# Decoder trunk: keys first where attention begins, DVE and ACT in a written order there, and one weight scaling tied behind the last branch readings

## The chip, the core and the metric

The kernel runs on one core of a Trainium2 chip. The metric is device time of one execution in microseconds (us). Five engines run their own instruction streams and wait for each other by semaphores: PE (TensorE, matmuls), DVE (VectorE), ACT (ScalarE), POOL (GpSimd) and SP (SyncE, which issues most of the DMAs).

## The reference, cut to what matters

One layer on x of 512 x 1024, in float32:

```python
h = _rmsnorm(x, norm1_g[l]) * (1.0 + scale1) + shift1
proj = h @ w_in[l]
qa, ka, va, qd, kd, vd, ga, gd = jnp.split(proj, points, axis=-1)
out_a = _sliding_window_attention(qa, ka, va, sinks, slopes_swa)      # 8 heads, 2 key heads, window 128
out_b = _diff_attention(qd, kd, vd, lam, lam_init, subln_g, slopes_diff)
merged = sigmoid(ga) * (out_a @ w_branch_swa) + sigmoid(gd) * (out_b @ w_branch_diff)
x = x + gate1 * (merged @ w_out)
x = x + gate2 * _conv_ffn(rmsnorm2(x), ...)                           # gated MLP, causal convolution
out = _rmsnorm(x, final_g)
```

(The call of attention and the lines from `merged` on are shortened here.)

## The kernel before

Every float32 operand of a projection is split in two parts that PE multiplies fast: a high part, which ACT makes as a cast, and a low part, which DVE makes as a subtraction of the high part from the original (`split`, L104; `evac`, L399). A product then takes three matmuls (high by high, high by low, low by high). For weights, `split_pair` (L97) takes a raw tile of 128 x 1024 and gives `_h` and `_l` out of small rings of buffers; a new raw load waits until an earlier raw tile has been split.

**The first projection** (`mm_k`, L344, `product`, L333) runs over eight blocks k of the model dimension. PE keeps eight sums of 128 x 512 in its eight PSUM banks all the while: the keys `aka` (0), two of the four query sums `aqa0` (1) and `aqa1` (2), the differential values `av0` (3), `av1` (4), `av2` (6) and `av3` (7), and the sliding-window values `ava` (5). In the last k the three matmuls of each sum stand together, so that the sums are complete one after the other, in the order of the tuple in `mm_k`.

**Reading the sums out.** `keep_v(i)` splits one value sum into `vvh` (ACT) and `vvl` (DVE). Keys and queries are 64 wide, and two heads lie in one sum, in its lower and upper 64 partitions. They are stored so that scores are two matmuls over 128 partitions: `stack` (L410) puts a query's high part into its own half of `qa` (ACT, L415) and the low part into the other half (DVE, L418); for `ka`, each half holds high parts twice (L443, four ACT casts) and a low part twice (L445, two DVE subtractions, then L448, two ACT copies). `vaT` (L449) is a plain copy. A stretch between `man.enter_context(tc.manual_schedule(...))` and `man.close()` keeps the written order on DVE and ACT; elsewhere a scheduler sets it from its estimate and from priorities, and `tc.issue_after(x)` keeps what is written inside it behind x.

**What PE does there.** PE's order is written out: `fill(n)` (L483) runs n steps of a queue of projections, three matmuls each, and between them stand scores (`swa_scores`, L524, named `sw`), transposes and value products. The first two projections in the queue are the other two query sums (`add_q`, L599; matmuls L108 to L110, sums `pqa2` and `pqa3`, weights `wqa2` and `wqa3`), then heads of the differential attention (`pq0` with `w2_0`). `SWA_FILL` (L36) says how many steps stand in each gap. A score's maximum is taken by DVE (L545, `mx`), the softmax is ACT's (L557 to L560), its divisor DVE's, `pva` (L459) transposes `vaT` in a bank that a value sum held. `nm` (L556) is the maximum, scaled, that the exponentials need.

**The output projection.** Each branch is multiplied by its weights in `add_merge` (L893); the sum of the differential branch is `pB0` to `pB7`, and DVE reads it in L913 (`tdall`), adds the other branch (L914) and splits the result into `mg..h` and `mg..l`. The output projection's eight sums `oc` (L1186 to L1190) take over banks, one of them that of `pB7`. Its weights `wo0` to `wo7` come through `load_rows` (L958): a load, a scaling by the gate on DVE (L961) and a split.

Of the kernel before, what the change touches and what calls it, by code (L numbers as in the profile page):

```python
# [8 lines left out]
F32 = mybir.dt.float32  # L9
F32R = mybir.dt.float32r  # L10
AF = mybir.ActivationFunctionType
# [3 lines left out]
P = 128  # L15
# [17 lines left out]
STAT_LAG = 10  # L33
NORM_LAG = 16
VA_AT = 5
SWA_FILL = (1, 2, 6, 2, 2, 2, 2, 3)  # L36
DIFF_FILL = (3, 2, 4, 2)
NCOL = 161

# [4 lines left out]
def kernel(  # L44
# [47 lines left out]
    def raw_tile(shape, name):  # L92
        return wp.tile(shape, F32, tag="raw", bufs=4, name=name)
# [250 lines left out]
    def mm_k(k, part):  # L344
        if k < KT - 1:
            for i in (3, 4, 6, 0, 1, 2, 5, 7) if k < 2 else range(8):
                product(k, i, part)
        elif part == 0:
            for i in (3, 0, 1, 5, 2, 4, 6, 7):
                for p in range(3):  # L350
                    product(k, i, p)

# [54 lines left out]

    halves = ((lower, upper), (upper, lower))

    def stack(dst, src, scale, js=(0, 1), soon=True):  # L410
        with tc.high_priority(offset=HP) if soon else ExitStack():
            sc = [scale if isinstance(scale, float) else scale[own] for own, _ in halves]
            for j in js:
                own = halves[j][0]
                nc.scalar.activation(dst[own, j], src[own], AF.Copy, scale=sc[j])  # L415
            for j in js:
                own, other = halves[j]
                nc.vector.scalar_tensor_tensor(  # L418
                    dst[other, j], src[own], sc[j], dst[own, j].bitcast(F32), ALU.mult, ALU.subtract
                )  # L420
# [10 lines left out]
    vv = [big.tile([P, DIFF_HEADS, S], F32R, tag=f"vv{g}", name=f"vv{g}") for g in "hl"]  # L431
    vaT = big.tile([P, S], F32, tag="sq2", name="vaT")

    def keep_v(i):
        t = TOKENS[i] * P
        evac(*(v[:, :, t : t + P] for v in vv), acc[i].rearrange("p (h d) -> p h d", d=P))

    man = ExitStack()
    man.enter_context(tc.manual_schedule(engines={nc.vector.engine, nc.scalar.engine}))
    keep_v(3)  # L440
    for j, (own, other) in enumerate(halves):
        for to in (own, other):
            nc.scalar.copy(ka[to, j, 0], acc[0][own])  # L443
    for j, (own, _) in enumerate(halves):
        nc.vector.tensor_sub(ka[own, j, 1], acc[0][own], ka[own, j, 0].bitcast(F32))  # L445
    stack(qa[:, 0], acc[1], qsc[:, 0:1])
    for j, (own, other) in enumerate(halves):
        nc.scalar.copy(ka[other, j, 1], ka[own, j, 1])  # L448
    nc.scalar.copy(vaT, acc[5])  # L449
    man.close()  # L450
    stack(qa[:, 1], acc[2], qsc[:, 1:2], soon=False)
    keep_v(4)
    keep_v(6)
    keep_v(7)

    def turn_va():
        pv = tbank("pva")
# [6 lines left out]
        nsink = cpool.tile([P, 8], F32, name="nsink")  # L464
        nc.vector.tensor_scalar_mul(nsink, sink, -1.0)


    def load_tile(n, name):
        r = raw_tile([P, KT, P], name)
        nc.sync.dma_start(r, w_tiles[n])  # L470
        return split_pair(r, [P, KT, P], name)

    man = ExitStack()
    man.enter_context(tc.manual_schedule(engines={nc.tensor.engine}))
# [124 lines left out]
    def add_q(i):  # L599
        def q(wts):  # L600
            o = fbank(f"pqa{i}")
            yield from steps(o, wts, hT, KT)
            stack(qa[:, i], o, qsc[:, i : i + 1])

        units.append((lambda: load_tile(TILE_QA + i, f"wqa{i}"), q))

    def add_head(h):
        def q(wts):
# [155 lines left out]

    pairs, firsts, scored, probs, aTs = {}, {}, {}, {}, {}
    ada = ada_rows()
    add_q(2)
    add_q(3)
    add_head(0)
    add_head(1)  # L770
    with tc.issue_after(tiles[KT - 1].ins):
        prefetch(1)
        fill(SWA_FILL[0])
    swa_scores(0, 0)
    with tc.issue_after(pairs[0].last.ins):
# [89 lines left out]
    tds = {}  # L865

    g1b = gpart(4, [P, D], "g1b")
    g1c, s2c, a2c, g2c = (late_mod[:, 8 * i : 8 * i + 8] for i in range(4))
# [24 lines left out]
    def add_merge(j):  # L893
# [14 lines left out]
        def branch(wts):  # L908
            o = sbank(f"pB{j}")
            rhs = [[vv[b][:, k] for k in range(4)] for b in range(2)]  # L910
            yield from steps(o, wts, rhs, 4, cl=slice(j % 2 * P, j % 2 * P + P))
            td = tds[j]
            nc.vector.scalar_tensor_tensor(td, td, 1.0, o, ALU.add, ALU.mult)  # L913
            nc.vector.tensor_add(td, td, ta[:, j])  # L914
            split(mgh[j], mgl[j], td)

# [887 lines left out]
```

## Time and profile before

| | us |
|---|---|
| median of 3 runs (lowest, highest) | 684.09 (683.17, 686.54) |
| the profiled execution | 684.12 |
| its span | 682.3 |
| PE busy | 670.2 |
| DVE busy | 567.7 |
| ACT busy | 403.7 |

The profile is one execution on the chip. The span runs from the first to the last recorded instruction. A timeline row reads: start in us, duration in us, engine, line of the kernel, operation, output<-input, and, in brackets, how long the engine stood idle before it and whose work ended that. A row with x4 stands for four instructions of one kind in a row. Names are cut of their numbers in the trace (`wqa` is `wqa2` or `wqa3`). Matmuls are pipelined, so that one starts before the last has ended: what a matmul costs is read from the distance between starts.

### The profile page before, as it was taken

The page shows a single profiled execution, that of the slowest core. Times are in us where ns is not written, and L with a number is a line of the kernel's source. Part 1 is how long each engine was busy: PE and PEld are TensorE (multiplying, and loading weights), DVE is VectorE, ACT ScalarE, POOL GpSimd, SP SyncE. Part 2 cuts the span into 40 slices and gives each one's busy share as a digit, 9 for nine tenths or more (in the row PEclk, how much of TensorE's full clock was granted, in tenths as well). Part 3 has the DMA queues.
Part 4 walks back from the last instruction along what each step waited for, and adds up shares of the span by engine and source line. Part 5 has one row for each costly group of instructions (what it writes and reads, how often), then busy time and mean ns, then how long its engine had stood idle before and what let it go on. Part 6 is the DMA issues. An engine that isn't in the chain of part 4 may idle for free.

```text
span 682.3 us, 10835 instructions
## 1 busy us (share of the span) xinstructions
PE 670.2 (98%) x4053; PEld 594.3 (87%) x4053; DVE 567.7 (83%) x1049; ACT 403.7 (59%) x703; POOL 66.1 (10%) x74
## 2 busy tenths in 40 slices
PE   8999999999999999999999999999999999999995
PEld 7887787888888888878899999999999998888884
DVE  5986887789887388973689998888888999979997
ACT  6678878565654233332498565565556666656665
POOL 2000000001000000000020120111110003440300
PEclk9999999999999999999999999999999999999998
DMA  9961322354254289757473998787867658996903
GB/s 359 418 218 35 124 62 94 123 155 130 93 180 155 80 291 304 263 128 270 144 125 97 215 218 213 185 194 178 215 159 189 149 185 189 195 204 188 166 1 124
DMA packets 71077, 119.68 MB, mean 175 GB/s; under 512 B 3952, under 2 KB 47728, under 8 KB 71024
## 3 DMA queue, kind: packets, MB, share of 16 engines
q1 hardware_dynamic: 52960, 95.04, 41.7%
q0 software_dynamic: 17776, 23.60, 21.4%
q8 instruction: 32, 0.52, 0.3%
q10 hardware_dynamic: 288, 0.34, 0.2%
q14 instruction: 21, 0.17, 0.1%
HBM read 116.87 MB, written 2.10 MB: 174 GB/s over the span
## 4 chain that ended last, share of the span: by engine, by line
PE 79%; DVE 8%; DMA 6%; issue 3%; ACT 3%; ACTq 0%; DVEq 0%
PE up L1130 33%; PE dc L1733 11%; DMA wgd<-in_w_tiles_dram 3%; PE av L342 3%; DMA wo<-in_w_out_dram 2%; PE oc L1186 2%; PE oc L1187 2%; PE oc L1190 2%; PE pga L108 2%; PE pga L110 2%; PE pga L109 2%; PE sd L637 2%; PE aqa L339 1%; PE pq L108 1%; PE pk L108 1%
## 5 line engine op out<-in xcount | busy, mean ns | idle before, releaser
L1130 PE MATMUL up<-t,m_whi 128*128 128x256 f32 x512 | 93.1, 283 | 0.0
L1130 PEld LDWEIGHTS up<-t,m_whi 128*128 128x128 f32 x512 | 79.9, 192 | 0.0
L1130 PE MATMUL up<-t,m_wlo 128*128 128x256 f32 x256 | 72.4, 283 | 0.0
L1130 PE MATMUL up<-bh,p_whi 128*128 128x256 f32 x232 | 65.7, 283 | 0.0
L1130 PE MATMUL up<-bl,p_whi 128*128 128x256 f32 x232 | 65.7, 283 | 0.0
L1130 PE MATMUL up<-bh,p_wlo 128*128 128x256 f32 x232 | 65.7, 283 | 0.0
L1130 PEld LDWEIGHTS up<-t,m_wlo 128*128 128x128 f32 x256 | 49.2, 192 | 0.0
L1130 PEld LDWEIGHTS up<-bh,p_whi 128*128 128x128 f32 x232 | 44.5, 192 | 0.0
L1130 PEld LDWEIGHTS up<-bl,p_whi 128*128 128x128 f32 x232 | 44.5, 192 | 0.0
L1130 PEld LDWEIGHTS up<-bh,p_wlo 128*128 128x128 f32 x232 | 44.5, 192 | 0.0
L1033 POOL DMA_DIRECT2D s<-in_w_up_dram x21 | 27.0, 1365 | 158.2 <-DMA s<-in_w_up_dram 110.3
L1061 ACT CAST m_whi<-s 128x1024 fp32r<-128x1024 f32 x31 | 32.4, 1046 | 15.7 <-DVE s L1055 9.1
L732 DVE CUSTOM_DVE_ANT_0 ra<-ra,csb 128x1024 f32<-128x1024 f32 x32 | 38.6, 1221 | 1.6 <-DMA ra<-in_w_ada_t_dram 1.5
L1065 DVE TENSOR_TENSOR m_wlo<-s,m_whi 128x1024 fp32r<-128x1024 f32 x31 | 37.8, 1219 | 1.3 <-ACT m_whi L1061 1.3
L1130 PE MATMUL up<-t,p_whi 128*128 128x256 f32 x176 | 32.2, 283 | 0.0
L662 ACT ACTIVATE sd<-sd,dmx 128x128 f32<-128x128 f32 (+3 forms) x32 | 17.8, 557 | 20.7 <-DVE dmx L660 16.5
L1130 PEld LDWEIGHTS up<-t,p_whi 128*128 128x128 f32 x176 | 27.4, 192 | 0.1
L1061 ACT CAST p_whi<-wa 128x1024 fp32r<-128x1024 f32 x18 | 18.8, 1042 | 12.6 <-PE up L1130 5.4
L141 POOL TENSOR_TENSOR r<-ms,mhalf 128x4 f32<-128x4 f32 x4 | 5.3, 1323 | 215.5 <-DVE ms L137 215.5
L1137 ACT ACTIVATE gT<-a,cols 128x512 f32<-128x512 f32 x22 | 17.6, 812 | 13.4 <-DVE a L1172 13.0
L1065 DVE TENSOR_TENSOR p_wlo<-wa,p_whi 128x1024 fp32r<-128x1024 f32 x18 | 22.0, 1223 | 4.0 <-ACT p_whi L1061 3.8
L1130 PE MATMUL up<-t,p_wlo 128*128 128x256 f32 x88 | 24.9, 283 | 0.0
(519 smaller groups left out, 2055.7 us busy)
## 6 DMA issues: line engine op xcount, KB each, us to landing
ra<-in_w_ada_t_dram SPq DMA_DIRECT2D x32, 512.0 KB, 4.0
wa<-in_w_up_dram SPq DMA_DIRECT2D x22, 512.0 KB, 4.2
s<-in_w_up_dram SPq DMA_DIRECT2D x21, 512.0 KB, 4.5
s<-in_w_up_dram POOLq DMA_DIRECT2D x21, 512.0 KB, 7.2
adaw<-in_w_ada_t_dram SPq DMA_DIRECT2D x15, 512.0 KB, 10.0
a<-in_w_up_dram SPq DMA_DIRECT2D x11, 512.0 KB, 4.9
b<-in_w_down_dram SPq DMA_DIRECT2D x10, 512.0 KB, 4.0
w<-in_w_first_dram SPq DMA_DIRECT2D x8, 512.0 KB, 9.9
```

The costliest lines, as they stand in the source:

```text
L108: nc.tensor.matmul(o, lh, rh, start=start, stop=False)
L109: nc.tensor.matmul(o, lh, rl, start=False, stop=False)
L110: nc.tensor.matmul(o, ll, rh, start=False, stop=stop)
L342: nc.tensor.matmul(acc[i], ht[:, t : t + P], wts[k][w][:, S:], start=start, stop=stop)
L662: nc.scalar.activation(pm[m], pm[m], AF.Exp, bias=mx[:, m : m + 1], scale=slope, accum_out=lsum[:, m : m + 1])
L732: nc.vector.tensor_tensor_reduce(r, r, csb, 1.0, 0.0, ALU.mult, ALU.add, late_mod[:, idx : idx + 1])
L1033: nc.gpsimd.dma_start(dst, upblock(*blk), accum_op=ALU.add)
L1061: nc.scalar.copy(W[J, name][0], R[J, SRC[name]])
L1065: nc.vector.tensor_sub(lo, R[J, SRC[name]], hi.bitcast(F32))
L1130: nc.tensor.matmul(o[u], w[:, k, cu], b[:, k], start=name in ("p1", "m5", "p2") and k == 0 and x == 0, stop=k == 3 and x == 2, skip_group_ ...
L1137: nc.scalar.activation(grow(j), av[J][:, u], AF.Identity, bias=cv[:, 66 + j : 67 + j], scale=cv[:, 44 + j : 45 + j])
L1733: nc.tensor.matmul((bank2[u] if o is None else o)[:, sl], a[:, q, cu], b[:, q, sl], start=first_mm and x == 0, stop=last_mm and x == 2, sk ...
```

## The change

In the last k of the first projection the keys come before `av0`. The manual stretch on DVE and ACT begins with the loads and splits of `wqa2` and `wqa3`, and then gives the order of each key, query and value step one by one: keys' first high parts, `av0`, the first queries between the rest of the keys, the high parts of the second queries, of `av2`, then `vaT`. One key cast moves from ACT to DVE. The low parts of the second queries and of the values `av1` to `av3` are written behind the first softmax. `SWA_FILL` has one step more ahead of the first scores and one less behind them. At the output projection, the load and scaling of `wo6` are tied behind the last two branch readings.

```diff
-SWA_FILL = (1, 2, 6, 2, 2, 2, 2, 3)
+SWA_FILL = (2, 1, 6, 2, 2, 2, 2, 3)
...
-            for i in (3, 0, 1, 5, 2, 4, 6, 7):
+            for i in (0, 3, 1, 5, 2, 4, 6, 7):
...
-    def stack(dst, src, scale, js=(0, 1), soon=True):
+    def stack(dst, src, scale, soon=True, high=True, low=True):
...
-    def keep_v(i):
+    def keep_v(i, parts=(0, 1)):
         t = TOKENS[i] * P
-        evac(*(v[:, :, t : t + P] for v in vv), acc[i].rearrange("p (h d) -> p h d", d=P))
+        hi, lo = (v[:, :, t : t + P] for v in vv)
+        src = acc[i].rearrange("p (h d) -> p h d", d=P)
+        if 0 in parts:
+            nc.scalar.copy(hi, src)
+        if 1 in parts:
+            nc.vector.tensor_sub(lo, src, hi.bitcast(F32))
...
     man = ExitStack()
     man.enter_context(tc.manual_schedule(engines={nc.vector.engine, nc.scalar.engine}))
+    first_tiles = [load_tile(TILE_QA + i, f"wqa{i}") for i in (2, 3)]
+    nc.scalar.copy(ka[lower, 0, 0], acc[0][lower])
+    nc.scalar.copy(ka[upper, 1, 0], acc[0][upper])
+    nc.vector.tensor_sub(ka[lower, 0, 1], acc[0][lower], ka[lower, 0, 0].bitcast(F32))
+    nc.vector.tensor_sub(ka[upper, 1, 1], acc[0][upper], ka[upper, 1, 0].bitcast(F32))
     keep_v(3)
-    for j, (own, other) in enumerate(halves):
-        for to in (own, other):
-            nc.scalar.copy(ka[to, j, 0], acc[0][own])
-    for j, (own, _) in enumerate(halves):
-        nc.vector.tensor_sub(ka[own, j, 1], acc[0][own], ka[own, j, 0].bitcast(F32))
-    stack(qa[:, 0], acc[1], qsc[:, 0:1])
-    for j, (own, other) in enumerate(halves):
-        nc.scalar.copy(ka[other, j, 1], ka[own, j, 1])
-    nc.scalar.copy(vaT, acc[5])
+    nc.scalar.activation(qa[lower, 0, 0], acc[1][lower], AF.Copy, scale=qsc[lower, 0:1])
+    nc.vector.scalar_tensor_tensor(
+        qa[upper, 0, 0], acc[1][lower], qsc[lower, 0:1], qa[lower, 0, 0].bitcast(F32), ALU.mult, ALU.subtract
+    )
+    nc.scalar.copy(ka[upper, 0, 0], acc[0][lower])
+    nc.scalar.copy(ka[upper, 0, 1], ka[lower, 0, 1])
+    nc.scalar.activation(qa[upper, 0, 1], acc[1][upper], AF.Copy, scale=qsc[upper, 0:1])
+    nc.vector.tensor_copy(ka[lower, 1, 0], acc[0][upper])
+    nc.vector.tensor_sub(ka[lower, 1, 1], acc[0][upper], ka[lower, 1, 0].bitcast(F32))
+    nc.vector.scalar_tensor_tensor(
+        qa[lower, 0, 1], acc[1][upper], qsc[upper, 0:1], qa[upper, 0, 1].bitcast(F32), ALU.mult, ALU.subtract
+    )
+    stack(qa[:, 1], acc[2], qsc[:, 1:2], soon=False, low=False)
+    keep_v(6, (0,))
+    vat_copy = nc.scalar.copy(vaT, acc[5])
     man.close()
-    stack(qa[:, 1], acc[2], qsc[:, 1:2], soon=False)
-    keep_v(4)
-    keep_v(6)
-    keep_v(7)
+    keep_v(4, (0,))
+    keep_v(7, (0,))
...
-    add_q(2)
-    add_q(3)
+    for i in (2, 3):
+        add_q(i)
+        loaded.append((first_tiles[i - 2], units.pop()[1]))
...
-    with tc.issue_after(tiles[KT - 1].ins):
-        prefetch(1)
+    with tc.issue_after(vat_copy.ins):
         fill(SWA_FILL[0])
-    swa_scores(0, 0)
-    with tc.issue_after(pairs[0].last.ins):
-        fill(SWA_FILL[1])
-        swa_scores(0, 2)
-    with tc.issue_after(pairs[0].last.ins):
+        swa_scores(0, 0)
+        with tc.issue_after(pairs[0].last.ins):
+            fill(SWA_FILL[1])
+            swa_scores(0, 2)
+    with tc.issue_after(pairs[0].last.ins), tc.issue_after(vat_copy.ins):
         swa_softmax(0)
+        keep_v(6, (1,))
+        stack(qa[:, 1], acc[2], qsc[:, 1:2], high=False)
+        keep_v(4, (1,))
+        keep_v(7, (1,))
...
-            nc.vector.scalar_tensor_tensor(td, td, 1.0, o, ALU.add, ALU.mult)
+            merged.append(nc.vector.scalar_tensor_tensor(td, td, 1.0, o, ALU.add, ALU.mult))
...
-    with tc.issue_after(recent[0].ins), tc.issue_after(recent[1].ins):
-        wo = [load_rows(wout, 0, "wo0", g1b)]
-    wo += [load_rows(wout, k, f"wo{k}", g1b) for k in range(1, KT)]
+    wo = []
+    for k in range(KT):
+        with ExitStack() as place:
+            for b in recent if k == 0 else merged[-2:] if k == 6 else ():
+                place.enter_context(tc.issue_after(b.ins))
+            wo.append(load_rows(wout, k, f"wo{k}", g1b))
```

(In the parts left out, `stack` runs over its two halves as before, each part only where `high` or `low` asks for it, `load_tile` is defined earlier, and `add_q` takes no loader.)

Where the engines' rows move: ACT first, from the end of the first projection to the first softmax. Before:

```order
L105 CAST wqa2_h_618<-wqa2_616 128x1024
L105 CAST wqa3_h_653<-wqa3_651 128x1024
L105 CAST w2_0_h_720<-w2_0_718 128x1024
L401 CAST vvh_580<-av0_141 128x4x128
L443 CAST ka_577<-aka_138 64x512 x4
L415 ACTIVATE qa_576<-aqa0_139,qsc_148 64x512 x2
L448 COPY ka_577<-ka_577 64x512 x2
L449 COPY vaT_582<-ava_143 128x512
```

and of the change, at the same place:

```order
L105 CAST wqa3_h_593<-wqa3_591 128x1024
L451 CAST ka_577<-aka_138 64x512
L452 CAST ka_577<-aka_138 64x512
L439 CAST vvh_580<-av0_141 128x4x128
L456 ACTIVATE qa_576<-aqa0_139,qsc_148 64x512
L460 CAST ka_577<-aka_138 64x512
L461 COPY ka_577<-ka_577 64x512
L439 CAST vvh_580<-av1_142 128x4x128
L462 ACTIVATE qa_576<-aqa0_139,qsc_148 64x512
L415 ACTIVATE qa_576<-aqa1_140,qsc_148 64x512 x2
L439 CAST vvh_580<-av2_144 128x4x128
L470 COPY vaT_582<-ava_143 128x512
```

The cast of `wqa2` now stands four rows earlier, ahead of the last block's `hThB`; that of `w2_0` stands behind `vaT` and the cast of `av3`. Three of the four key casts and one of the two low copies are left on ACT.

DVE at the same place, from the split of `wqa` to the first scores' maxima (L545, in the change L559). Before:

```order
L105 TENSOR_TENSOR wqa2_l_619<-wqa2_616,wqa2_h_618 128x1024
L402 TENSOR_TENSOR vvl_581<-av0_141,vvh_580 128x4x128
L445 TENSOR_TENSOR ka_577<-aka_138,ka_577 64x512 x2
L418 SCALAR_TENSOR_TENSOR qa_576<-aqa0_139,qsc_148,qa_576 64x512 x2
L545 ISA st0_0_630,mx0_626<-sw0_0_0_634,dsw_157 128x128
L545 ISA mx0_626 128x1
L545 ISA st0_1_631,mx0_626<-sw0_0_0_634,dsw_157 128x256
L545 ISA mx0_626 128x1
L418 SCALAR_TENSOR_TENSOR qa_576<-aqa1_140,qsc_148,qa_576 64x512
```

and of the change:

```order
L105 TENSOR_TENSOR wqa3_l_594<-wqa3_591,wqa3_h_593 128x1024
L453 TENSOR_TENSOR ka_577<-aka_138,ka_577 64x512
L454 TENSOR_TENSOR ka_577<-aka_138,ka_577 64x512
L441 TENSOR_TENSOR vvl_581<-av0_141,vvh_580 128x4x128
L457 SCALAR_TENSOR_TENSOR qa_576<-aqa0_139,qsc_148,qa_576 64x512
L463 CAST ka_577<-aka_138 64x512
L464 TENSOR_TENSOR ka_577<-aka_138,ka_577 64x512
L465 SCALAR_TENSOR_TENSOR qa_576<-aqa0_139,qsc_148,qa_576 64x512
L559 ISA st0_0_634,mx0_630<-sw0_0_0_638,dsw_157 128x128
```

The low part of `wqa3` came behind the maxima and three `vvl` before; it now stands with that of `wqa2` ahead of the keys. The two low parts of the second queries (`aqa1`), which stood between the maxima of the first pair, and the `vvl` of `av2`, `av1` and `av3` follow behind all maxima, next to the two `nm`.

DVE where the output projection begins. Before:

```order
L105 TENSOR_TENSOR mg3l_2365<-tdall_2366,mg3h_2364 128x512
L961 TENSOR_TENSOR wo6_2930<-wo6_2930,g1b_2367 128x1024
L913 SCALAR_TENSOR_TENSOR tdall_2366<-tdall_2366,pB7_2836 128x512
L105 TENSOR_TENSOR m5w_2963<-s1_t1_2956,m5w_2963 128x1024
L914 TENSOR_TENSOR tdall_2366<-tdall_2366,ta_1235 128x512
```

and of the change:

```order
L105 TENSOR_TENSOR mg3l_2365<-tdall_2366,mg3h_2364 128x512
L931 SCALAR_TENSOR_TENSOR tdall_2366<-tdall_2366,pB7_2836 128x512
L979 TENSOR_TENSOR wo6_2930<-wo6_2930,g1b_2367 128x1024
L932 TENSOR_TENSOR tdall_2366<-tdall_2366,ta_1235 128x512
L105 TENSOR_TENSOR m5w_2963<-s1_t1_2956,m5w_2963 128x1024
```

The reading of the last branch sum has passed the scaling of `wo6`. On PE, the last products of `aka` and `av0` have changed places and three matmuls of `pqa2` have moved ahead of the first scores; the orders of POOL and SP are as before.

More of the change, by code (lines that the diff above doesn't have):

```diff
@@ L408 @@
     halves = ((lower, upper), (upper, lower))
-    def stack(dst, src, scale, js=(0, 1), soon=True):
+    def stack(dst, src, scale, soon=True, high=True, low=True):
         with tc.high_priority(offset=HP) if soon else ExitStack():
             sc = [scale if isinstance(scale, float) else scale[own] for own, _ in halves]
-            for j in js:
+            for j in range(2) if high else ():
                 own = halves[j][0]
                 nc.scalar.activation(dst[own, j], src[own], AF.Copy, scale=sc[j])
-            for j in js:
+            for j in range(2) if low else ():
                 own, other = halves[j]
@@ L432, with load_tile @@
     vaT = big.tile([P, S], F32, tag="sq2", name="vaT")
-    def keep_v(i):
+    def keep_v(i, parts=(0, 1)):
         t = TOKENS[i] * P
-        evac(*(v[:, :, t : t + P] for v in vv), acc[i].rearrange("p (h d) -> p h d", d=P))
+        hi, lo = (v[:, :, t : t + P] for v in vv)
[4 more added lines that the diff above has]
+            nc.vector.tensor_sub(lo, src, hi.bitcast(F32))
+    def load_tile(n, name):
+        r = raw_tile([P, KT, P], name)
+        nc.sync.dma_start(r, w_tiles[n])
+        return split_pair(r, [P, KT, P], name)
@@ L465 @@
         nc.vector.tensor_scalar_mul(nsink, sink, -1.0)
[L468 to L471, printed above, removed]
     man = ExitStack()
@@ L603, in q @@
             stack(qa[:, i], o, qsc[:, i : i + 1])
-        units.append((lambda: load_tile(TILE_QA + i, f"wqa{i}"), q))
+        units.append((None, q))
     def add_head(h):
@@ L864 @@
     tdall = gpart(2, [P, 3, S], "tdall")
-    tds = {}
+    tds, merged = {}, []
     g1b = gpart(4, [P, D], "g1b")
```

## The prediction

> **What bounds the kernel now.** The page first, for the busiest engine.
>
> ```profile
> span 682.3 us, 10835 instructions
> PE 670.2 (98%) x4053; PEld 594.3 (87%) x4053; DVE 567.7 (83%) x1049; ACT 403.7 (59%) x703; POOL 66.1 (10%) x74
> ```
>
> TensorE works for 670.2 of 682.3 us, and the change keeps every matmul. So it can gain only what PE loses, some 12 us in all. Two views say where: PE's waits, and the busy time by stretch (span in us, then PE busy first).
>
> ```profile
> PE oc L1186 <- DVE tdall L913: 1.3, 1, 1.3
> PE sw L540 <- DVE mx L545: 0.5, 1, 0.5
> ```
>
> ```profile
> 70.00:80.00 10.00, 10.00 (x62) 7.93 (x62) 9.57 (x36) 7.10 (x16) 0.00 (x0) 1.00 0.50 159
> 310.00:640.00 330.00, 330.00 (x2342) 311.48 (x2341) 286.74 (x415) 200.98 (x307) 54.73 (x47) 1.00 0.77 183
> ```
>
> The longest wait, 1.3 us, lies at the output projection; one of 0.5 lies where attention begins, and smaller ones stand in brackets below. From 70 to 80 and from 310 to 640 us PE never stops: what comes earlier there only shifts. The two places are the two parts of the change.
>
> **Part 1, attention's start, PE's side.** PE's timeline (start, duration; the bracket is the wait):
>
> ```profile
> 53.57 0.39 PE L342 MATMUL av<-whi,hThB 128*128 128x512 f32 x1
> 59.01 0.39 PE L108 MATMUL pqa<-hThA,wqa_h 128*128 128x512 f32 x1
> 59.87 0.72 PE L540 MATMUL sw<-ka,qa 128*128 128x128 f32 x4
> 60.75 0.70 PE L540 MATMUL sw<-ka,qa 128*128 128x128 f32 x4 [0.15 <-DVE qa L418]
> 61.29 0.40 PE L108 MATMUL pqa<-hThA,wqa_h 128*128 128x512 f32 x1
> 62.66 0.63 PE L540 MATMUL sw<-ka,qa 128*128 128x256 f32 x4
> 63.78 0.74 PE L540 MATMUL sw<-ka,qa 128*128 128x256 f32 x4 [0.48 <-DVE mx L545]
> 64.36 0.40 PE L108 MATMUL pqa<-hThA,wqa_h 128*128 128x512 f32 x1
> 67.79 0.60 PE L459 MATMUL pva<-ident,vaT 128*128 128x128 f32 x4
> 68.14 0.48 PE L108 MATMUL pqa<-hThA,wqa_h 128*128 128x512 f32 x1
> 69.24 0.50 PE L110 MATMUL pqa<-hThA,wqa_l 128*128 128x512 f32 x1 [0.39 <-DVE wqa_l L105]
> 69.58 1.09 PE L540 MATMUL sw<-ka,qa 128*128 128x128 f32 x8
> ```
>
> Starts show the cost better than durations, which overlap. Six pqa matmuls from 61.29 to 62.66 are 0.228 each; four scores 0.54 to 0.58 (60.75 to 61.29, 63.78 to 64.36); pva 0.35; the three pqa behind it 0.78 without a wait (0.34 from 69.24 to 69.58 for the last). From 59.01 to 69.58 the same work without a stop is 24 x 0.228 + 8 x 0.135 + 8 x 0.145 + 0.35 + 0.78 = 8.84 of 10.57: **1.73 us are lost**, more than the waits view lists. They go at 59.87 (0.18), between the first scores (0.34), at 63.78 (0.54) and at 69.24 (0.66).
>
> Now the rows that make PE late, ACT's and then DVE's.
>
> ```profile
> 48.18 0.82 ACT L328 ACTIVATE hThB<-xT,mod 128x512 fp32r<-128x512 f32 x1
> 54.72 0.58 ACT L401 CAST vvh<-av 128x512 fp32r<-128x512 f32 x1
> 55.20 2.37 ACT L443 CAST ka<-aka 64x512 fp32r<-64x512 f32 x4
> 57.59 1.38 ACT L415 ACTIVATE qa<-aqa,qsc 64x512 fp32r<-64x512 f32 x2
> ```
>
> ```profile
> 57.60 1.41 DVE L445 TENSOR_TENSOR ka<-aka,ka 64x512 fp32r<-64x512 f32 x2 [1.57 <-ACT ka L443]
> 59.08 1.53 DVE L418 SCALAR_TENSOR_TENSOR qa<-aqa,qsc,qa 64x512 fp32r<-64x512 f32 x2
> 62.32 0.74 DVE L418 SCALAR_TENSOR_TENSOR qa<-aqa,qsc,qa 64x512 fp32r<-64x512 f32 x1 [0.93 <-ACT qa L415]
> 65.22 0.42 DVE L545 CUSTOM_DVE_ANT_0 st<-sw,dsw 128x256 f32<-128x256 f32 x1
> 66.17 1.88 DVE L402 TENSOR_TENSOR vvl<-av,vvh 128x512 fp32r<-128x512 f32 x3
> 67.97 1.21 DVE L105 TENSOR_TENSOR wqa_l<-wqa,wqa_h 128x1024 fp32r<-128x1024 f32 x1
> ```
>
> Today DVE idles 1.57 us until the fourth key cast leaves ACT at 57.57; then keys' and queries' low parts take it to 60.6. The later qa at 62.32 stands between the first scores' maxima, which holds PE at 63.78. The second wqa low part waits behind three vvl until 67.97, which holds PE at 69.24.
>
> **After, worked forward on the old clock.** The key sum's last products take the three slots from 53.57, so keys are complete 0.68 earlier, at 54.4. ACT is free by then, since both wqa casts stand ahead and the cast of w, which sat in front of the keys, moves behind the values. Prices: on ACT a 64-row cast 0.59 (2.37/4), a qa activation 0.70, vvh and vaT 0.5 to 0.59; on DVE a ka subtraction 0.71, a qa low part 0.76, a vvl 0.60 to 0.69, a maximum of 256 columns 0.35 to 0.42. The one operation the trace doesn't show is DVE's cast of a key half. The nearest row:
>
> ```profile
> L253 DVE COPY csb<-aka x1: 691/691/691, 6.5 to 6.5; 128x512 f32<-128x512 f32 x1
> ```
>
> It is a copy of the same length out of the same sum: 0.69. Its ends are 0.42, the pass over 256 columns, and 0.76, the longest pass over 512; I take 0.69, the row that does the same thing.
>
> ACT: two casts 54.45 to 55.62, vvh 56.1, qa 56.8, DVE's second subtraction awaited, ka 57.10 to 57.68 and its low copy to 58.3, vvh, qa 59.5, two qa 60.9, vvh, vaT 62.0, vvh, the w cast to 63.5. DVE: subtractions 55.66 to 57.06, vvl 57.77, qa low 58.44, cast 59.16, subtraction 59.9, qa low 60.69. ACT, DVE, ACT and DVE now alternate on the key sum; each handover is taken at what ACT to DVE shows (57.57 to 57.60): 0.03. The cast of keys that moved from ACT to DVE costs DVE 0.69, and its cover is PE's three earlier pqa (0.68): without them the scores would wait 0.2.
>
> PE: six pqa instead of three stand ahead of the scores, 59.01 to 60.38. The first scores need the subtraction of 59.9 and, for their second half (60.92), the qa low of 60.69: **no wait**, by 0.5 and 0.2. Scores to 61.46, three pqa to 62.14, the next scores to 63.30: their maxima are no longer behind a qa low, so the 0.54 goes. Fifteen pqa to 66.72. Here the moved work comes back: DVE ends the maxima at 64.3, nm at 64.5, two qa lows at 66.0, nm, and two vvl at 66.8 and 67.45. The transposes pva take the bank that the first vvl empties (0.10 of wait), the next pqa that of the second. The second pair's scores start at 66.72 + 0.10 + 0.35 + 0.28 + 0.78 = 68.23 for 69.58: **1.35 us**, with 0 and 1.73 as ends. The second wqa's low part, late by 0.66 today, is then long done.
>
> Behind it, the first softmax follows on ACT at 64.6 for 66.17 and ends by 68.8; the scalings that the transposes of 70.5 need are done on DVE at 69.6. The split of w, now behind all this, ends on DVE at about 75.1; PE wants it 1.35 earlier than today, at 77.30.
>
> ```profile
> 78.65 0.39 PE L110 MATMUL pq<-hThA,w_l 128*128 128x512 f32 x1
> ```
>
> The ties to vaT's copy (62.0) only set an order: what they hold, nm and the low parts, comes after 64.3 anyway. SP and POOL keep their order; two loads that wait for wqa's raw buffers can go out earlier, and nothing of PE's hangs on them before 70.
>
> The new early places cost nothing as long as their loads are in. ACT's cast of wqa now stands ahead of the last hThB (48.18) and pushes it and its low part to 51.4; PE wants these at 53.57 and, two matmuls on, 54.02.
>
> ```profile
> L470 SPq DMA_DIRECT2D wqa<-in_w_tiles_dram x2: 327/328/328, 34.8 to 39.4; - x2
> DMA to landing us min/median/max: 3.9/5.2/6.5
> ```
>
> The later load is in by 39.4 + 6.5 = 45.9 at the latest, 2.3 ahead of the cast.
>
> One rule of the Trainium skill bears on the alternation, "PSUM — Partial Sum Buffer", section "PSUM bank collisions raise a hardware error": two engines collide on one bank only within a quadrant of 32 partitions, while different quadrants may be read at once. This program waits by whole bank, as the trace shows: DVE starts at 57.60 when the last cast of either half is done. Were halves kept apart, DVE could begin one cast (0.59) earlier, the two late waits of 0.10 and 0.28 would vanish, and part 1 would give 1.73 for 1.35; the rows speak for the bank.
>
> **Part 2, the output projection.** DVE's rows, then PE's:
>
> ```profile
> 299.91 0.69 DVE L105 TENSOR_TENSOR mg3l<-tdall,mg3h 128x512 fp32r<-128x512 f32 x1 [0.69 <-ACT mg3h L105]
> 301.24 1.23 DVE L961 TENSOR_TENSOR wo<-wo,g1b 128x1024 f32<-128x1024 f32 x1 [0.64 <-DMA wo<-in_w_out_dram]
> 302.39 0.68 DVE L913 SCALAR_TENSOR_TENSOR tdall<-tdall,pB 128x512 f32<-128x512 f32 x1
> ```
>
> ```profile
> 297.74 0.39 PE L110 MATMUL pB<-vvh,wbd 128*128 128x512 f32 x1
> 301.16 0.61 PE L1190 MATMUL oc<-wo_h,mg0l 128*128 128x512 f32 x2
> 303.12 0.50 PE L1186 MATMUL oc<-wo_h,mg0h 128*128 128x512 f32 x1 [1.34 <-DVE tdall L913]
> ```
>
> The last branch reading (L913) frees a bank that PE needs. Its operands were there at 298.1, but it stands behind a scaling that waits for its own load. Moved ahead, it runs at 300.6 to 301.25; PE is there at 301.16 + 0.46 = 301.62, 0.37 later. The whole 303.12 - 301.62 = **1.50 us** goes. The scaling starts at 301.25 for 301.24, its load still the later; the wo6 it makes is used near the projection's end.
>
> That holds if DVE's chain comes 1.35 earlier too. It does if PE paces it:
>
> ```profile
> 228.12 0.39 PE L109 MATMUL pga<-hTlB,wga_h 128*128 128x512 f32 x1
> ```
>
> ```profile
> 228.59 1.05 ACT L105 CAST wgd_h<-wgd 128x1024 fp32r<-128x1024 f32 x1 [7.53 <-issue]
> ```
>
> This cast sat idle for 7.53 us and starts as PE's last matmul with the weight half whose slot it takes is over (228.12 + 0.39, 228.59); from there loads, splits and scalings follow each other to 302.
>
> **Sum.** The profiled run took 684.12, 1.82 around its span; the median shown is 684.09, so nothing has to be shifted. 684.12 - 1.35 - 1.50 = **681.27 us**. What a measurement of this kernel can tell from no change is about 0.5%, 3.4 us: the forecast lies inside.
>
> **Rivals.**
> 1. *The first wait only changes its name.* DVE's work ahead of the first scores grows by a cast and a vvl; if its seven steps cost 0.15 more each, 1.05 in all, the first scores wait until 60.95, the maxima, qa lows and vvl follow by as much, and 0.3 of 1.35 is left: 682.3. For it: margins of 0.5 and 0.2. Against: every price is a row's.
> 2. *DVE's chain to 302 doesn't move with PE,* because loads pace it. Then PE comes at 300.27 and waits for 301.25: 1.87 in all, 682.25. Against it stands the cast released by PE.
> 3. *The gain is given back,* a later tile being wanted before it is split: 683.5 to 684.5. The w split has 2.2 us to spare, and PE has no wait to 300.
> 4. *Slower.* The wqa cast ahead of the last hThB waits for its load. If that lands after 48.18 + (54.02 - 51.4) = 50.8, PE stops one for one in the middle of the projection; past 50.8 + 2.85 = 53.65 it is slower than before, past 57.1 by over 0.5%: 684 to 688. Landing at 45.9 at the latest speaks against it.
>
> **How the numbers follow.** Forecast 0.64, own range 680.5 to 682.0; rival 1 0.13; rival 2 0.10; rival 3 0.07; rival 4 0.06. The low end, 680.0, is both parts at their most (1.73 and 1.50 make 680.9) and the scatter of a median; the high end, 684.3, takes in rivals 1 and 2 and half of 3. Left out are rival 4, the rest of 3 and tails, some 0.17. Faster by over 0.5% means below 680.7: 0.14, from the forecast's lower part. Slower by as much needs 687.5: 0.05. Within: 0.81.
>
> **What would show it.** Right: no wait of PE at sw, at most 0.3 at pva and pqa, the first score near 60.4, sw of the second pair near 68.2, no oc wait, that matmul near 300.3. Rival 1: a wait of sw for ka or qa. Rival 2: oc still waiting 1 us for tdall. Rival 4: PE waiting for hThB or hTlB near 54. A mistake in how I carried DVE through 64 to 67 us would show in the wait of pva.

## The result and the profile after

| | before | after |
|---|---|---|
| median (lowest, highest), 9 runs each | 683.67 (683.17, 686.54) | 681.04 (680.57, 681.9) |
| ratio of times, 95% interval | | 0.9958 (0.9948 to 0.9969) |
| the profiled execution | 684.12 | 681.18 |
| its span | 682.3 | 679.4 |

The change makes the kernel 0.4% faster: 681.04 us against a forecast of 681.3. The interval leaves out 1, so the gain is small but clear of no change. The page of the kernel after, its span and its engines:

```profile
span 679.4 us, 10834 instructions
PE 669.8 (99%) x4053; PEld 595.4 (88%) x4053; DVE 569.0 (84%) x1051; ACT 402.0 (59%) x701; POOL 66.0 (10%) x74
```

PE works as long as before; what went is idle time. PE's waits, all that the view lists:

```profile
PE ava L219 <- POOL ones L116: 1.1, 1, 1.1
PE av L289 <- DVE sq L299: 0.4, 1, 0.4
PE pva L478 <- DVE vvl L441: 0.4, 1, 0.4
PE av L342 <- ACT hThA L328: 0.2, 1, 0.2
```

The waits of `oc` (1.3), of `sw` (0.5) and of `pqa` (0.4) are gone, and one is new: `pva` waits for a `vvl`. The same shows in busy time by stretch (span, then PE busy first). From 70 to 80 us and from 310 to 640 PE is busy throughout, as before, and now also from 230 to 310, where the output projection begins (78.66 of 80 before):

```profile
70.00:80.00 10.00, 10.00 (x64) 8.00 (x63) 8.44 (x33) 7.23 (x19) 0.00 (x0) 1.00 0.26 81
...
230.00:310.00 80.00, 80.00 (x364) 66.43 (x363) 62.89 (x86) 29.30 (x39) 1.49 (x1) 1.00 0.76 250
310.00:640.00 330.00, 330.00 (x2342) 311.61 (x2342) 288.62 (x419) 201.33 (x309) 55.38 (x47) 1.00 0.78 181
```

Attention's start in PE's timeline:

```profile
59.45 0.39 PE L108 MATMUL pqa<-hThA,wqa_h 128*128 128x512 f32 x1
60.81 1.25 PE L554 MATMUL sw<-ka,qa 128*128 128x128 f32 x8
61.90 0.39 PE L108 MATMUL pqa<-hThA,wqa_h 128*128 128x512 f32 x1
62.60 1.10 PE L554 MATMUL sw<-ka,qa 128*128 128x256 f32 x8
63.54 0.40 PE L108 MATMUL pqa<-hThA,wqa_h 128*128 128x512 f32 x1
66.75 0.39 PE L110 MATMUL pqa<-hThB,wqa_l 128*128 128x512 f32 x1
67.56 0.63 PE L478 MATMUL pva<-ident,vaT 128*128 128x128 f32 x4 [0.42 <-DVE vvl L441]
68.06 0.50 PE L108 MATMUL pqa<-hThA,wqa_h 128*128 128x512 f32 x1
68.86 1.09 PE L554 MATMUL sw<-ka,qa 128*128 128x128 f32 x8
69.78 0.40 PE L108 MATMUL pqa<-hThA,wqa_h 128*128 128x512 f32 x1
```

Eight scores now stand together twice (x8) where before they were broken by waits that the view lists. The first eight still hold a shorter wait: they take 61.90 - 60.81 = 1.09, the second pair's eight 69.78 - 68.86 = 0.92. From the first `pqa` to the second pair's scores it is 68.86 - 59.45 = 9.41 us for 10.57: 1.16 less.

A ledger of milestones in PE's starts shows where the rest lies. Its columns are the first product of the first projection (start), and then the distances from there to the first `pqa`, to the second pair's scores (`sw`), to the first `pq`, to the first `oc`, to the `oc` matmul that waited, and to the end of the span. The rows from the fourth on are experiments, explained below.

| | start | to pqa | to sw | to pq | to oc | to that oc | rest | span |
|---|---|---|---|---|---|---|---|---|
| before | 15.18 | 43.83 | 10.57 | 8.62 | 220.56 | 4.36 | 379.18 | 682.3 |
| before, again | 15.19 | 43.86 | 10.57 | 8.58 | 220.57 | 3.67 | 379.16 | 681.6 |
| after | 15.63 | 43.82 | 9.41 | 8.25 | 220.57 | 2.86 | 378.86 | 679.4 |
| after, again | 14.98 | 43.83 | 9.43 | 8.22 | 220.98 | 2.85 | 378.91 | 679.2 |
| tie only | 15.59 | 43.82 | 10.57 | 8.62 | 220.53 | 2.86 | 378.91 | 680.9 |
| start only | 15.49 | 43.80 | 9.42 | 8.25 | 220.59 | 3.78 | 379.07 | 680.4 |
| start only, again | 15.27 | 43.83 | 9.41 | 8.25 | 220.81 | 3.14 | 379.09 | 679.8 |
| fill back | 15.08 | 43.82 | 10.12 | 8.24 | 220.53 | 2.85 | 378.96 | 679.6 |
| cast on ACT | 15.32 | 43.83 | 10.23 | 8.25 | 220.56 | 2.86 | 378.85 | 679.9 |
| keys third | 15.35 | 43.80 | 10.10 | 8.25 | 220.64 | 2.85 | 378.91 | 679.9 |
| wqa3 late | 15.65 | 43.83 | 11.37 | 8.22 | 220.58 | 2.87 | 378.88 | 681.4 |
| values first | 15.32 | 43.84 | 8.67 | 8.50 | 220.67 | 2.86 | 378.94 | 678.8 |
| va copy first | 15.55 | 43.83 | 8.67 | 8.35 | 220.92 | 2.86 | 378.92 | 679.1 |
| all four | 15.49 | 43.82 | 8.67 | 8.35 | 220.94 | 2.86 | 378.87 | 679.0 |

From before to after: start +0.45, `sw` -1.16, `pq` -0.37, the waiting `oc` -1.50, rest -0.3: -2.9 in all. The first number is no work of the change: the start lies between 14.98 and 15.65 in all fourteen profiles, and two profiles of one kernel, the change itself, are 0.65 apart.

### The profile page after: what moved, and what is told of

Its sections match the earlier page's. It is cut to its first block, busy times and chain, and to the rows that moved or that the text cites. A ratio compares the mean times of both kernels' runs of the same rounds, so it can differ in the third digit from the quotient of the medians.

```text
span 679.4 us, 10834 instructions
## 1 busy us (share of the span) xinstructions
PE 669.8 (99%) x4053; PEld 595.4 (88%) x4053; DVE 569.0 (84%) x1051; ACT 402.0 (59%) x701; POOL 66.0 (10%) x74
## 4 chain that ended last, share of the span: by engine, by line
PE 93%; DVE 5%; issue 1%; ACT 1%; POOL 0%; DVEq 0%; ACTq 0%; POOLq 0%
PE up L1151 33%; PE dc L1754 11%; PE av L342 3%; PE pga L108 2%; PE pga L110 2%; PE pga L109 2%; PE oc L1207 2%; PE pgd L108 2%; PE oc L1211 2%; PE pgd L109 2%; PE oc L1208 2%; PE pgd L110 2%; PE aqa L339 2%; PE sd L651 2%; PE pq L108 1%; PE pk L108 1%
```

## The experiments

Each verdict uses the stretch that the edit touches. Medians of one kernel differ by some tenths between measurements (the kernel before: 683.07 to 683.77), the three short stretches by a few hundredths, and the long one to `oc` by up to 0.4.

**The two parts apart.** The kernel before with the tie alone:

```diff
+            merged.append(nc.vector.scalar_tensor_tensor(td, td, 1.0, o, ALU.add, ALU.mult))
+            for b in recent if k == 0 else merged[-2:] if k == 6 else ():
+                place.enter_context(tc.issue_after(b.ins))
```

> The kernel before with the tie of wo6 behind the last two branch readings alone. Two independent parts: the 1.34 us wait of oc for tdall goes and nothing else moves, 1.50 us less than before's 683.67, so 682.2, with the waits of 0.5 (sw for mx) and 0.4 (pqa for wqa_l) still there. Rival, loads pace that place and the wait only changes its name (oc waiting for wo or mg instead): 683.4 to 683.7.

Measured: 682.62 (12 runs), ratio 0.9986 (0.9977 to 0.9994). PE's waits where the change has taken them away:

```profile
PE sw L540 <- DVE mx L545: 0.5, 1, 0.5
PE pqa L110 <- DVE wqa_l L105: 0.4, 1, 0.4
```

`oc` is no longer on the list and its distance is 2.86, as in the change; attention's start keeps both its waits and its 10.57. So the tie alone takes the `oc` wait away. But the median fell by 0.82 (683.44 for the kernel before, measured beside it), not by 1.5.

The change without the tie:

```diff
-            for b in recent if k == 0 else merged[-2:] if k == 6 else ():
+            for b in recent if k == 0 else ():
```

> The changed kernel without the tie of wo6: attention's start alone. Two independent parts: oc waits for tdall again, 1.3 to 1.5 us, and the time is 681.04 + 1.5 = 682.5, 1.1 to 1.5 under before. Rival, DVE's chain to 302 doesn't follow PE: oc waits 2.4 us or more and the gain of the start is gone, 683.3 to 683.7.

Measured: 682.46 (12 runs), ratio 0.9981 (0.9963 to 1.0), 0.98 under the same 683.44. By medians alone that is not clear of no change, but its 9.42 and 8.25 are those of the change. DVE and PE where the output projection begins:

```profile
299.45 1.23 DVE L979 TENSOR_TENSOR wo<-wo,g1b 128x1024 f32<-128x1024 f32 x1 [0.56 <-DMA wo<-in_w_out_dram]
300.59 0.68 DVE L931 SCALAR_TENSOR_TENSOR tdall<-tdall,pB 128x512 f32<-128x512 f32 x1
```

```profile
301.33 0.50 PE L1207 MATMUL oc<-wo_h,mg0h 128*128 128x512 f32 x1 [0.76 <-DVE tdall L931]
```

The order is that of before, scaling ahead of reading, and the wait is back, but it costs 3.78 - 2.86 = 0.92, not 1.50. Two causes were open: the earlier start of attention makes the wait shorter, or the wait is another in each execution, because the scaling waits for a load. One more profile each of this kernel and of the kernel before tells them apart.

> The changed kernel without the tie of wo6, a second look. If the wait of oc for tdall (0.92 us from starts in e2, 1.50 before) is set by when the loads of that execution land, it differs again by some tenths, with the distance from the cast of wgd to the scaling of wo6 (72.07 in e2, 72.65 before). If the earlier start shrinks it, it is 0.9 again at 72.1.

> The kernel before, a second look. By the loads: the wait of oc is another than 1.50 by some tenths and follows the distance from the cast of wgd to the scaling of wo6. By the start: 1.50 again at 72.65. The stretch from the first pqa to the second pair's scores is 10.57 by either.

Measured: 681.64 and 683.34. The kernel before, its DVE row and PE's wait in the second profile:

```profile
300.57 1.23 DVE L961 TENSOR_TENSOR wo<-wo,g1b 128x1024 f32<-128x1024 f32 x1 [0.53 <-DMA wo<-in_w_out_dram]
```

```profile
302.44 0.50 PE L1186 MATMUL oc<-wo_h,mg0h 128*128 128x512 f32 x1 [0.65 <-DVE tdall L913]
```

The loss against 2.86 is 1.50 and 0.81 in the kernel before, 0.92 and 0.28 without the tie. PE arrives at the same point within 0.02 us in both profiles of before (15.18 and 15.19 at the start, 220.56 and 220.57 later), and the scaling starts at 301.24 and 300.57. The time from the cast of `wgd` at 228 to the start of that scaling is 301.24 - 228.59 = 72.65 and 71.96 in before, 72.07 and 71.42 without the tie, and the loss is that less 71.15 in all four. Both kernels show a long and a short wait, so the earlier start doesn't decide it; the chain of loads does, and in every kernel with the tie the distance is 2.85 to 2.87.

**The steps of part 1, one undone at a time.** Fill back:

```diff
-SWA_FILL = (2, 1, 6, 2, 2, 2, 2, 3)
+SWA_FILL = (1, 2, 6, 2, 2, 2, 2, 3)
```

> The changed kernel with one step of pqa ahead of the first scores and two behind, as before. If that step is the cover of the keys' longer chain on DVE, the first scores wait 0.3 for ka and 0.2 for qa, everything behind comes 0.55 later and the time is 681.6. Rival, DVE's chain starts earlier with the scores and the wait at pva shrinks by as much: 681.0.

Measured: 681.74, ratio 0.9973 (0.9962 to 0.9983). PE's row:

```profile
60.04 1.49 PE L554 MATMUL sw<-ka,qa 128*128 128x128 f32 x8 [0.30 <-DVE ka L464]
```

With three matmuls less ahead of them, the first scores wait for the last key subtraction: 10.12 for 9.41, 0.71 lost. So the three `pqa` are the cover of that chain, at nearly their own length (3 x 0.228 = 0.68), and not the 0.55 that was expected.

Cast on ACT, the key cast back on its old engine:

```diff
-    nc.vector.tensor_copy(ka[lower, 1, 0], acc[0][upper])
+    nc.scalar.copy(ka[lower, 1, 0], acc[0][upper])
```

> The changed kernel with the fourth key cast back on ACT, behind the second half of the first queries. If the place of that cast decides when keys are ready, ACT makes it near 60.5, the subtraction ends 0.8 later than with DVE, the first scores wait 0.4 to 0.5 for ka and then for qa, and the time is 681.04 + 0.75 = 681.8. Rival, DVE's load is what counts and the 0.69 taken from it is gained: 680.4 to 680.7.

Measured: 681.71, ratio 0.9972 (0.9962 to 0.9983). PE's rows:

```profile
61.01 0.72 PE L554 MATMUL sw<-ka,qa 128*128 128x128 f32 x4 [0.34 <-DVE ka L464]
61.89 0.70 PE L554 MATMUL sw<-ka,qa 128*128 128x128 f32 x4 [0.16 <-DVE qa L465]
```

10.23, 0.82 lost, where 0.75 was expected: ACT reaches that cast only behind its other work, and keys and queries are both late.

Keys third, the old order in the last block of the projection:

```diff
-            for i in (0, 3, 1, 5, 2, 4, 6, 7):
+            for i in (3, 0, 1, 5, 2, 4, 6, 7):
```

> The changed kernel with the last key products behind those of av0 again, so keys are complete 0.68 later. Theory: the chain on the key sum starts that much later, the margins of 0.38 and 0.13 at the first scores are used up, and 0.3 to 0.55 is lost: 681.4 to 681.6, with a wait of sw for ka. Rival, the margins hold or the wait at pva absorbs it: 681.0.

Measured: 681.63, ratio 0.9968 (0.9956 to 0.9981). PE's row:

```profile
60.96 1.49 PE L554 MATMUL sw<-ka,qa 128*128 128x128 f32 x8 [0.29 <-DVE ka L464]
```

10.10, 0.69 lost: the length of the three matmuls that the keys moved by, where 0.3 to 0.55 was expected. Each of these three steps is thus needed by itself; undoing any of them gives back 0.7 to 0.8 of part 1.

All three losses are larger than expected because the margin at the first scores was already used up in the change. The second four of these scores need the queries' low part from DVE. The change, with the fifth score as a row of its own, and then DVE's row with the cast on ACT:

```profile
60.47 0.75 DVE L465 SCALAR_TENSOR_TENSOR qa<-aqa,qsc,qa 64x512 fp32r<-64x512 f32 x1
61.37 0.30 PE L554 MATMUL sw<-ka,qa 128*128 128x128 f32 x1
```

```profile
60.99 0.76 DVE L465 SCALAR_TENSOR_TENSOR qa<-aqa,qsc,qa 64x512 fp32r<-64x512 f32 x1
```

The fifth score starts 61.37 - 61.22 = 0.15 behind the end of that operation in the change, and 61.89 - 61.75 = 0.14 with the cast on ACT, where the view names it as what PE waited for. It is 0.15 in all fourteen profiles. So PE's place here hangs on DVE in every one: the fifth score stands 1.92 behind the first `pqa` in the change, 2.74 with the cast on ACT and 2.60 with keys third, 0.82 and 0.68 later, which is what was lost. With fill back it stands at 1.93, with three `pqa` still to run that the change has run by then.

Wqa3 late, the load and split of the second query weights left to the scheduler, as before:

```diff
-    first_tiles = [load_tile(TILE_QA + i, f"wqa{i}") for i in (2, 3)]
+    first_tiles = [load_tile(TILE_QA + i, f"wqa{i}") for i in (2,)]
...
+    units[-1] = (lambda: load_tile(TILE_QA + 3, "wqa3"), units[-1][1])
```

> The changed kernel with the load and split of the second wqa left to the scheduler as before; it puts the split between the first pair's maxima. Theory: DVE waits there for ACT's cast (to about 64.0) and works until 65.2, the other maxima, nm and the values' low parts come 1.9 later, and pva waits that much more: 683.0. Rival, only the 0.66 that the late split cost before comes back: 681.7.

Measured: 684.12 (11 runs), ratio 0.9996 (0.9984 to 1.0009); the profiled execution took 683.16 at a granted clock of 0.996, the median one lists 0.994. PE's row:

```profile
69.48 0.63 PE L478 MATMUL pva<-ident,vaT 128*128 128x128 f32 x4 [2.31 <-DVE vvl L441]
```

The split now stands on DVE between the first four maxima and the other four (64.06 to 65.28), having waited 1.26 for ACT's cast, and `pva` waits 2.31: 11.37 for 9.41, more than before the change (10.57). The 1.96 is as expected.

**The wait that is left.** Values first puts the two `vvl` that free banks ahead of the second queries' low parts:

```diff
-        stack(qa[:, 1], acc[2], qsc[:, 1:2], high=False)
+        with tc.issue_after(vlow[4].ins):
+            stack(qa[:, 1], acc[2], qsc[:, 1:2], high=False)
```

> The changed kernel with the low parts of the values av2 and av1 ahead of the second queries' low parts on DVE. If what is left of the wait (0.42 us of pva for vvl, about 0.74 from starts) is only DVE's order, it goes: no wait of pva, second pair's scores 0.7 earlier, 680.3. Rival, the second pair's scores need the second queries' low parts just as early: a wait of sw for qa takes its place, 680.8 to 681.1.

Measured: 680.77, ratio 0.9956 (0.9944 to 0.9968). PE and ACT:

```profile
66.69 0.60 PE L480 MATMUL pva<-ident,vaT 128*128 128x128 f32 x4
67.83 1.08 PE L556 MATMUL sw<-ka,qa 128*128 128x128 f32 x8
70.12 1.19 PE L595 MATMUL tp<-ident,st 128*128 128x128 f32 x7
71.07 0.48 PE L108 MATMUL pqa<-hThA,wqa_h 128*128 128x512 f32 x1
```

```profile
68.74 1.37 ACT L415 ACTIVATE qa<-pqa,qsc 64x512 fp32r<-64x512 f32 x2
70.13 0.59 ACT L481 COPY va<-pva 128x512 f32<-128x512 f32 x1
```

The wait of `pva` is gone and the second pair's scores come 0.74 earlier. Then the transposes, which take 0.68 by starts in the change (71.18 to 71.86), take 0.95 here: ACT copies `pva` out only at 70.13, and PE now comes to a bank that isn't free. 0.25 of the 0.74 is given back before the first `pq` (8.50 for 8.25), and the median is 680.8, as the rival had it, though for another wait than the rival's: 2.67 under before here, 2.63 for the change in its own runs.

Va copy first keeps that edit and puts ACT's copy of `pva` ahead of the third queries' high parts, whose low parts go behind the second pair's maxima:

```diff
-        nc.scalar.copy(va.rearrange("p t d -> p (t d)"), pv)
+        with tc.high_priority(offset=HP):
+            c = nc.scalar.copy(va.rearrange("p t d -> p (t d)"), pv)
+        with tc.issue_after(c.ins):
+            held[0](low=False)
...
+                with tc.issue_after(pairs[1].last.ins):
+                    held[0](high=False)
```

> The kernel with the values' low parts first (e3), and besides, ACT copies pva before the third queries' high parts, and DVE takes the second pair's maxima before the third queries' low parts. Theory: in e3 the gain of 0.74 was half given back to a wait of the transposes for ACT's copy of pva (0.27) and of the next scores for maxima (0.1); both go, 0.35 under e3: 680.4, 0.6 under the changed kernel. Rival, what e3 gave back is lost elsewhere: 680.8 to 681.0.

Measured: 680.86, ratio 0.9955 (0.9942 to 0.9967). PE, DVE and ACT (of ACT's two copies, the first alone):

```profile
98.04 0.40 PE L110 MATMUL pq<-hThA,w_l 128*128 128x512 f32 x1
98.56 0.87 PE L598 MATMUL tp<-ident,st 128*128 128x128 f32 x6
```

```profile
97.02 0.66 DVE L402 TENSOR_TENSOR outal<-oa,outah 128x512 fp32r<-128x512 f32 x1
97.59 1.07 DVE L587 TENSOR_SCALAR st<-st,lsum 128x128 f32<-128x128 f32 x4
```

```profile
97.92 0.59 ACT L600 COPY pT<-tp 128x512 f32<-128x512 f32 x1
```

Of the 0.25 that was given back before the first `pq`, 0.15 is regained (8.35), but the later transposes at 98.56 start 0.29 late: PE was ready 0.23 behind 98.04, at 98.27. The stretch to `oc` is 220.92, and the median is that of values first, not the 680.4 expected. On DVE, `outal` stands ahead of the scalings that feed them, so the last kernel ties it behind those:

```diff
+        if i == 1:
+            nc.scalar.copy(outa[0][:, i], o)
+            with tc.issue_after(pairs[2].end.ins):
+                nc.vector.tensor_sub(outa[1][:, i], o, outa[0][:, i].bitcast(F32))
```

> The kernel of e8, and the low part of the second pair's output (outal, 0.66 us on DVE) tied behind the third pair's last scaling. Theory: e8 lost 0.35 at the third pair's second transpose, which waited for scalings behind outal; that goes, from PE's third queries to the output projection the stretch is 220.56 again, and the time is 0.55 to 0.65 under the changed kernel: 680.4. Rival, the scheduler's order gives it back at another place: 680.8 to 681.0.

> The changed kernel once more, beside e9 on one chip: 681.0 within 0.3, and from the first pqa to the second pair's scores 9.41 us, from there to pq 8.25, by every theory. Where the first product of PE starts (15.63 in its first profile) can be anywhere from 15.1 to 15.7 if that is scatter of an execution and no effect of the change.

Measured on one chip (before 683.07 there): all four 680.37, ratio 0.9961 (0.9948 to 0.9975); the change again 681.00, ratio 0.9969 (0.9958 to 0.9981). All four, PE, DVE and ACT's first copy:

```profile
97.98 0.40 PE L110 MATMUL pq<-hThA,w_l 128*128 128x512 f32 x1
98.51 0.87 PE L598 MATMUL tp<-ident,st 128*128 128x128 f32 x6
```

```profile
97.08 1.08 DVE L587 TENSOR_SCALAR st<-st,lsum 128x128 f32<-128x128 f32 x4
```

```profile
97.87 0.58 ACT L600 COPY pT<-tp 128x512 f32<-128x512 f32 x1
```

The time came, its reason did not. The scalings start half a us earlier and the transposes still start 0.30 behind PE (98.51 for 98.21): `outal` was not the cause. What fits is ACT: the transposes take over the bank that the first of two copies `pT` frees, at 97.87 + 0.58 = 98.45; in the kernel ahead that is 97.92 + 0.59 = 98.51, and in values first 97.61 + 0.59 = 98.20. The transposes start 0.05 to 0.06 behind that in all three (98.51, 98.56, 98.25). That is argued from three profiles; no kernel with an earlier copy was run. Nor do the stretches give the 0.63 between the two medians: up to `oc` all four is ahead of the change's first profile by 0.74 - 0.10 - 0.37 = 0.27. That its time came as forecast is luck in part.

The change again came at 681.00, as expected; its start, 14.98, lies below the 15.1 that was taken as the lowest. It lost 0.41 in the stretch to `oc` (220.98), where one wait shows, `td` for DVE by 0.22 at 141.96. ACT's cast of `wga` had waited for its load until 136.75, and until 135.66 in the first profile. ACT's next exponentials come behind that cast, and DVE waits for them by 0.36 on its way to `td`. The first profile of the same kernel has no such loss, so it belongs to the execution, not to the kernel.

## Why the prediction was right

1. **The place of the gain.** Both waits that the sum rested on were on PE, and the listed ones went as told. The whole execution began 0.45 later, so 0.45 is to be taken off to compare with the forecast: the first scores start at 60.81 - 0.45 = 60.36 for 60.4, the `oc` matmul at 300.54 - 0.45 = 300.09 for 300.3.

2. **Part 1** was put at 1.35; 1.16 came at its place and 0.37 up to the first `pq`. Together that is 1.53. The sizes that missed, each by some tenths, partly cancel, so that the total comes near is luck in part. The wait left at `pva` and the next `pqa` was taken at 0.38; by starts it is 67.56 - 66.75 - 0.23 = 0.58 and 68.06 - 67.56 - 0.35 = 0.15, so 0.73; the listed 0.42 at `pva` is above the 0.3 that the prediction had set as a sign of being right. PE had come sooner: the second eight scores took 63.54 - 62.60 = 0.94 where 1.16 was taken, since the prices of 0.135 and 0.145 had been read from fours that stood behind waits (eight without one take 0.92, above). DVE came a little later:

```profile
64.91 1.51 DVE L418 SCALAR_TENSOR_TENSOR qa<-aqa,qsc,qa 64x512 fp32r<-64x512 f32 x2
66.72 1.29 DVE L441 TENSOR_TENSOR vvl<-av,vvh 128x512 fp32r<-128x512 f32 x2
```

   The order of these rows is the one worked out. The first `vvl` ends near 66.72 + 0.69 = 67.41, and PE takes its bank over at 67.56: a handover of 0.15 that the sum had at nothing. The prediction had named this place as its weakest. What was gained further on, 0.37, was in no step: most of it is a wait inside a row of several matmuls. Eight scores of the kernel before and after, each with the matmul behind them:

```profile
74.84 1.43 PE L540 MATMUL sw<-ka,qa 128*128 128x256 f32 x8
76.11 0.40 PE L108 MATMUL pqa<-hThA,wqa_h 128*128 128x512 f32 x1
```

```profile
74.00 1.20 PE L554 MATMUL sw<-ka,qa 128*128 128x256 f32 x8
75.04 0.40 PE L108 MATMUL pqa<-hThA,wqa_h 128*128 128x512 f32 x1
```

   They took 1.27 before and 1.04 after, while the busy time of that stretch is 10.00 of 10.00 in both. In the kernel before, the fifth of them starts at 75.53, 0.06 behind a maximum that DVE ends at 75.05 + 0.42 = 75.47, so a wait for the bank fits; it is argued from this one place. The prediction read "PE never stops" from the busy time, and so missed it.

3. **The unseen operation**, DVE's cast of a key half, was put at 0.69 between 0.42 and 0.76, and the alternation on the key sum at 0.03 for each handover. DVE and ACT after:

```profile
56.10 0.68 DVE L453 TENSOR_TENSOR ka<-aka,ka 64x512 fp32r<-64x512 f32 x1 [1.42 <-ACT ka L452]
59.02 0.69 DVE L463 CAST ka<-aka 64x512 fp32r<-64x512 f32 x1
```

```profile
55.48 0.58 ACT L452 CAST ka<-aka 64x512 fp32r<-64x512 f32 x1
57.52 0.58 ACT L460 CAST ka<-aka 64x512 fp32r<-64x512 f32 x1 [0.27 <-DVE ka L454]
```

   The cast took 0.69. DVE starts at 56.10, 0.04 after the second cast's end at 56.06, though it reads the half that was cast first; ACT waits for DVE's second subtraction and starts at 57.52. Halves are not kept apart, which is what the sum had; the prediction put that down to the bank of the sum, but both engines also write the tile `ka` there, and these rows can't tell the two apart. By the Trainium skill, "PSUM — Partial Sum Buffer", section "PSUM bank collisions raise a hardware error", halves of different quadrants could be read at once; these waits are the program's, and no run shows what the bank itself would do. Of the margins at the first scores, that of the keys held: the last key subtraction ends at 59.74 + 0.69 = 60.43, 0.38 ahead of PE. That of the queries, 0.2 in the sum, did not: the handover of 0.15 used it up, and the first eight scores hold the short wait shown above. So rival 1 fell by its size and not by its kind, and undoing any one step brings the wait of `sw` that it described, at 0.3.

4. **Part 2**, 1.50, came out to the hundredth against the profiled execution, and that overstates how well it was known. The wait is as long as one execution's loads make it: 1.50 and 0.81 in two profiles of before. The tie alone was worth 0.82 between medians. The wait also cost a little behind itself, which the sum left out: from the `oc` matmul that waited to the last one it is 41.66 and 41.65 in the two profiles of before, 41.47 after: 0.19, the larger part of the 0.3 in the last column but one of the ledger. Rival 2 fell as it was put: ACT's cast of `wgd` after:

```profile
227.51 1.05 ACT L105 CAST wgd_h<-wgd 128x1024 fp32r<-128x1024 f32 x1 [7.53 <-issue]
```

   It starts 227.51 - 77.11 = 150.40 behind the first `pq`, and 228.59 - 78.20 = 150.39 before, so DVE's chain moves with PE, as the release of that cast had said. From there on its length is the loads', as the rival had it.

5. **Rivals 3 and 4** left no trace in the pair of profiles: the stretches to `oc` and to the end are no longer than before, and PE has no wait for `hThB` near 54.

6. **The sum against the median.** The forecast took 684.12 as the level of the kernel before, and nine runs put it at 683.67. The profiled span fell by 2.9 and the median by 2.63, both near 2.85. That the spans agree so well is luck: the stretches behind the start fell by 3.35, half a us more than the sum, and a start that was 0.45 later took that back. Measured again, the medians are 683.07 and 681.00, 2.07 apart. And the parts alone, 0.82 and 0.98 by medians, add up to 1.80. The size of the whole gain is thus known to about half a us; that it lies at these two places is what the stretches show.

## What to carry to other kernels

When PE is busy 98% of the time, read its loss as distances between starts from one fixed matmul to the next: the short ones repeat within 0.06 us here, and they show waits that a row of eight matmuls hides. Take the price of a matmul from a place without a wait. A wait that hangs on a load has no one price: take it from several executions, or remove it with an order that doesn't ask for the load. A wait taken away brings PE sooner to the next bank that another engine still holds, which gave back 0.25 to 0.35 us twice here, so carry the forecast on to the next two handovers, with 0.05 to 0.15 us for each, and count a margin below that as none.

## What the runs showed of the hardware

- The first 15 us of identical code end anywhere from 14.98 to 15.65 in fourteen profiles, and the next 43.8 us repeat within 0.06.
- In the waits read here, PE started 0.05 to 0.06 or 0.14 to 0.15 us behind the end of DVE's or ACT's operation: `pva` 0.15 behind DVE's `vvl` (67.41 to 67.56), the fifth score 0.15 behind DVE's `qa` in all fourteen profiles, but `oc` 0.05 behind DVE's `tdall` (302.39 + 0.68 = 303.07 to 303.12). What decides between the two stays open. ACT and DVE handed over to each other in 0.03 to 0.04.
- The chain of loads, splits and scalings from the `wgd` cast to `wo6` took 71.4 to 72.7 us in four profiles without the tie, which moved one wait of PE between 0.28 and 1.50.
